# Closer steps for the second query group's norm, and an edge on the first head's key splits

## The chip, the cores and the metric

The kernel runs on one core of one Trainium2 chip. The metric is the device time of one execution in microseconds (us), and the comparison is with the same kernel before the change. The engines go by the profile's names: PE (TensorE, matmuls and transposes), PEld (its weight loads), DVE (VectorE), ACT (ScalarE), POOL (GpSimd) and SP (the queue that issues most transfers).

## What is computed

One layer of a hybrid encoder over 512 tokens and 16 meta tokens, width 2048, in float32. A projection of the normalised input feeds two mixers of eight heads each. Mixer B is differential attention with a distance penalty. Mixer A is grouped-query attention whose queries and keys are normalised per head and then turned by a rotary table. Cut to what matters here:

```python
hn = rmsnorm(h, pre_norm_g)
qa, ka, va, ga, qb, kb, vb, gb = split(hn @ w_in)
# mixer A: 8 query heads, 2 key heads
q = axial_rope(rmsnorm(heads_first(qa), q_norm_g), ang_row, ang_col)
k = axial_rope(rmsnorm(heads_first(ka), k_norm_g), ang_row, ang_col)
ya = softmax(q @ k.T / sqrt(128)) @ v * silu(ga)
yb = diff_attention(qb, kb, vb) * silu(gb)
out = h + rmsnorm(concat(ya, yb) @ w_out, post_norm_g)
```

## The kernel before

Every float32 operand is split into a high part (rounded to the matmul's input type) and a low part (the rest), and a product is three matmuls: high by high, low by high, high by low. `wsplit` (lines 155 to 161) does it for a block of 128x1024 weights: ACT writes `wh` (line 158), DVE writes `wl` (line 159). Blocks are fetched two ahead of the one in use, and each of `st`, `wh` and `wl` has three buffers, so the split of a block waits until PE has done with the block three before it. `hi` (line 322, ACT) and `lo` (line 325, DVE) do the same for activations.

PE's order is written out by the program itself. The dense projections form the main stream (`pd` tiles, and `po` tiles for the output projection). Attention heads are generators that the class `Lanes` (line 44) weaves into it. It keeps a clock that advances by an estimate of each matmul's time; a generator that yields x is taken up again when that clock has moved on by x. So a number after `yield` sets how many matmuls stand between two steps of a head, and through that where everything after it stands. `finish` runs a generator to its end at once, without other matmuls between, if it has not got there by then. On PE and SP the instructions stay in program order; on DVE, ACT and POOL a scheduler orders them, and each engine then takes them strictly one after the other.

Mixer A comes late. `queries_A(g)` (line 663) projects the queries of group g, four heads, into four token tiles `qn` (128 tokens by four heads by 128). For the second group, g = 1, the norm is the generator `later` (line 688): for each tile four squares with a sum on ACT (`jk`, line 596), then `rstd` on POOL (`ssq`, lines 243 and 245), and then for each tile on DVE four gain products (`gains`, line 601) and four operations of the rotation (`rope`, lines 618 to 623). They run while heads 2 and 3 of the first group are at work and while the gates `gA` are projected.

`attention_A(h)` (line 541) for the first head of the second group, h = 4, waits until that generator has ended (line 542). Then PE transposes the four tiles of the head (`tr<-ident,qn`, line 549), ACT and DVE split the result (`qh`, `qlA`), and four times PE computes scores (`sc`, line 566), DVE adds and takes the minimum (line 570), ACT takes the exponential (line 573) and POOL scales (line 575). `p_times_v` (line 414) transposes two blocks of scores (`tr<-ident,p`), splits them (`ph`, `pl`, `pm`) and multiplies with the values (`pv`). The transposes and `pv` share two PSUM banks, `sc` has one buffer. Heads 4 to 7 follow each other; the last is forced to its end at the last block of the first output projection (`dense_out(0)`, line 860), whose operand `oh15`, `ol15` is its result. The gate's SiLU (line 394) and the exponential need different tables on ACT, so each change between them has an ACT_TABLE_LOAD.

`keys_B` (line 327) of the first head of mixer B stands much earlier, behind the projection that opens the main stream (line 785): `halves` scales the keys, `hi` and `lo` split them into `s1` and `s2`.

Of the kernel before, what the change touches and what calls it, by code (L numbers as in the profile page):

```python
# [2 lines left out]

# [1 line left out]

# [5 lines left out]
F32 = mybir.dt.float32  # L11
F32R = mybir.dt.float32r
F16 = mybir.dt.float16
AF = mybir.ActivationFunctionType
ALU = mybir.AluOpType
# [16 lines left out]
LAG = dict(vals=3.5, bank=2.8, bankA=1.5, bankB=2.5, turnA=1.5, turnB=1.5, pvA=2.6, pvB=4.0, scB=3.0,  # L32
           pB=8.0, ss=6.0, qA=2.35, scA=5.4, pA=4.14, rope=10.2, head=3.85, fin=1.35, qn=1.4, norm=4.0)
# [75 lines left out]
def kernel(ctx: ExitStack, tc: tile.TileContext, xT, xn, xm, w_s, w_t, w_q, w_o,  # L109
                             gpre, gq, gk, lams, gsub, gpost, ident_d, cos_d, sin_d, dist_d, out):  # L110
    nc = tc.nc
# [43 lines left out]
    def wsplit(st, c=slice(0, 1024), ws=None):  # L155
        wh, wl = ws or [wp.tile([P, 1024], F32R, name=n, tag=n) for n in ("wh", "wl")]
        with tc.high_priority(rank[0]):
            nc.scalar.activation(wh[:, c], st[:, c], AF.Copy)  # L158
            nc.vector.tensor_tensor(out=wl[:, c], in0=st[:, c], in1=wh[:, c].bitcast(F32),  # L159
                                    op=ALU.subtract)  # L160
        return wh, wl

    rank = [AHEAD]

# [59 lines left out]
    first = [[pd.tile([P, 512], F32, name="pd", tag="pd") for _ in segs] for segs in start]  # L224
    for k0 in range(0, KT, 2):
        xload(k0)
        wh, wl = wload(w_s[k0 // 2], 768, load, 2 if k0 == 0 else 1)
        xload(k0 + 1)
        for k in (k0, k0 + 1):
            for i, (segs, pss) in enumerate(zip(start, first)):  # L230
                c = slice((i + 3 * (k - k0)) * P, (i + 3 * (k - k0) + 1) * P)
# [24 lines left out]
    for t in (TT, 0, 1, 2, 3):  # L256
        rows = P if t < TT else NM
        src = xn[t * P:(t + 1) * P, :] if t < TT else xm
        for j in range(2 if t < 2 else 4):
# [4 lines left out]
            st = ap.tile([P, w], F32, name="xns", tag=tag, bufs=2 if t < 2 else 4)[:rows]  # L264
# [54 lines left out]
    L, U = slice(0, 64), slice(64, 128)  # L319

    def hi(dst, src):
        nc.scalar.activation(dst, src, AF.Copy)  # L322

    def lo(dst, src, h):
        nc.vector.tensor_tensor(out=dst, in0=src, in1=h.bitcast(F32), op=ALU.subtract)  # L325

    def keys_B(pss):
        kf = ap.tile([P, NT], F32, name="kf", tag="tT")
        halves(pss, kf)
        s1 = ap.tile([P, NT], F32R, name="s1", tag="s1")  # L330
        s2 = ap.tile([P, NT], F32R, name="s2", tag="s2")
        hi(s1[L], kf[L])
        hi(s2[U], kf[U])
        lo(s1[U], kf[L], s1[L])
        lo(s2[L], kf[U], s2[U])
        return s1, s2

# [325 lines left out]
    def queries_A(g):  # L663

        pss = [pd.tile([P, 512], F32, name="pd", tag="pd") for _ in range(TT)]
        for k0 in range(0, KT, 2):
            wh, wl = fetch()

            for k, ts in [(k, h) for h in ((0, 1), (2, 3)) for k in (k0, k0 + 1)]:
                c = slice((k - k0) * 512, (k - k0 + 1) * 512)  # L670
                for t in ts:
                    ts_ = slice(NM + t * P, NM + (t + 1) * P)
                    mm(pss[t], xh[k][:, ts_], wh[:, c], start=(k == 0), stop=False)
                    mm(pss[t], xl[k][:, ts_], wh[:, c], start=False, stop=False)
                    mm(pss[t], xh[k][:, ts_], wl[:, c], start=False, stop=(k == KT - 1))
                    lanes.poll()
        res = []
        for t in range(TT):
            tag = "ql" if g == 0 else "fr" if t < 2 else "f"
            qn = ap.tile([P, 4, P], F32, name="qn", tag=tag, bufs=2 if tag == "fr" else 4)  # L680
            nc.scalar.activation(qn.rearrange("p n d -> p (n d)"), pss[t], AF.Copy,
                                 scale=rt[:, t:t + 1])
            res.append(qn)

        def last_of(engine):
            return next(i for i in reversed(nc.cur_bb.bb.instructions) if i.engine == engine)

        def later():

            ss = ap.tile([P, 16], F32, name="ssq", tag="ssq", bufs=1)  # L690
            for t, qn in enumerate(res):
                squares(qn, 4, ss[:, 4 * t:4 * t + 4])
                yield 2.0
            rstd(ss, ss, P)
            yield LAG["norm"]
            for t, qn in enumerate(res):
                with tc.issue_after(last_of(mybir.EngineType.DVE)):
                    gains(qn, 4, gqB, ss[:, 4 * t:4 * t + 4])
                    rope(qn, cosT[:, t:t + 1, :].broadcast_to([P, 4, P]),
                         sinT[:, t:t + 1, :].broadcast_to([P, 4, P]))  # L700
                yield LAG["norm"]

        def turn():
            if g == 1:
                yield from later()
                return
            for t, qn in enumerate(res):
                head_norm(qn, 4, gqB)
                rope(qn, cosT[:, t:t + 1, :].broadcast_to([P, 4, P]),
                     sinT[:, t:t + 1, :].broadcast_to([P, 4, P]))  # L710
                yield LAG["norm"]

        return res, lanes.spawn(turn(), 0.0)
# [69 lines left out]

    sc = psc.tile([P, 2, 512], F32, name="sc", tag="sc")
    pss = dense_T(KEYS, [sc[:, 0, :], sc[:, 1, :]], spread)
    ks = keys_B(first[0])
    qs = queries_B(0, first[1])
    v = values(pss)
    gB = [gate(first[2], "gB0")] + [None] * (NH - 1)
# [6 lines left out]
    for h in range(NH):  # L796
# [4 lines left out]
        if h + 1 < NH:  # L801
            if h:
                weigh()
            pss = dense_T(KEYS)
# [8 lines left out]
    for i in range(2):  # L813
        pss = dense_T(KEYS)
# [337 lines left out]
```

## Time and profile before

| what | value |
|---|---|
| median of 3 runs | 928.04 us (927.98 to 929.32) |
| the profiled execution | 927.7 us |
| its span (first to last instruction) | 925.9 us |
| mean granted clock of PE | 0.998 |
| busy: PE, DVE, ACT, POOL | 98%, 62%, 52%, 12% of the span |

In a row of the timeline the first number is the start in us from the span's start and the second the duration; "x4" means four instructions in one row, and brackets at the end name idle time before the row and what ended it. Matmuls are pipelined, so a matmul's duration is longer than its distance to the next one; distances between starts tell what PE's stream costs. In a row of windows the columns are: stretch, its length, busy time and number of instructions of PE, PEld, DVE, ACT and POOL, granted clock, share of the DMA engines, GB/s. In a row that groups a line's instructions the last numbers are busy us, mean ns of one, and idle time before them.

### The profile page before, as it was taken

The page shows a single profiled execution, that of the slowest core. Times are in us where ns is not written, and L with a number is a line of the kernel's source. Part 1 is how long each engine was busy: PE and PEld are TensorE (multiplying, and loading weights), DVE is VectorE, ACT ScalarE, POOL GpSimd, SP SyncE. Part 2 cuts the span into 40 slices and gives each one's busy share as a digit, 9 for nine tenths or more (in the row PEclk, how much of TensorE's full clock was granted, in tenths as well). Part 3 has the DMA queues.
Part 4 walks back from the last instruction along what each step waited for, and adds up shares of the span by engine and source line. Part 5 has one row for each costly group of instructions (what it writes and reads, how often), then busy time and mean ns, then how long its engine had stood idle before and what let it go on. Part 6 is the DMA issues. An engine that isn't in the chain of part 4 may idle for free.

```text
span 925.9 us, 14235 instructions
## 1 busy us (share of the span) xinstructions
PE 911.5 (98%) x5498; PEld 808.3 (87%) x5498; DVE 577.0 (62%) x1029; ACT 484.8 (52%) x847; POOL 114.1 (12%) x158
## 2 busy tenths in 40 slices
PE   9999999999999999999999999999999999899995
PEld 8999898998989899898999888888888888788884
DVE  6676675847567575765756247444755664564797
ACT  6464564638455474644655254437536753524652
POOL 0101010110101110010110020113101120300110
PEclk9999999999999999999999999999999999999999
DMA  9844534644536364232223223222222352676974
GB/s 340 286 137 140 148 113 113 156 130 142 143 108 178 93 169 137 69 104 69 91 64 98 91 91 91 69 80 80 73 88 68 121 157 80 230 218 185 298 305 182
DMA packets 43893, 128.11 MB, mean 138 GB/s; under 512 B 5105, under 2 KB 9073, under 8 KB 43569
## 3 DMA queue, kind: packets, MB, share of 16 engines
q1 hardware_dynamic: 40416, 115.66, 37.3%
q0 software_dynamic: 3264, 11.54, 6.6%
q8 instruction: 43, 0.70, 0.3%
q14 instruction: 26, 0.20, 0.1%
q10 hardware_dynamic: 144, 0.01, 0.0%
HBM read 118.80 MB, written 25.17 MB: 155 GB/s over the span
## 4 chain that ended last, share of the span: by engine, by line
PE 95%; DVE 3%; issue 0%; ACT 0%; POOL 0%; DVEq 0%
PE pd L63 61%; PE po L63 17%; PE sc L63 7%; PE pv L63 5%; PE tr L66 5%; DVE y L1041 1%; DVE wl L159 1%; PE hot L63 0%; PE ss L63 0%; DVE y L1053 0%; DVE y L1047 0%; DVE pl L325 0%; DVE l L325 0%; POOL p L490 0%; ACT ph L322 0%
## 5 line engine op out<-in xcount | busy, mean ns | idle before, releaser
L63 PE MATMUL pd<-xh,wh 128*128 128x264 f32 (+1 forms) x992 | 331.8, 335 | 0.0
L63 PE MATMUL pd<-xh,wl 128*128 128x264 f32 (+1 forms) x992 | 323.1, 326 | 1.2 <-DVE wl L159 1.2
L63 PE MATMUL pd<-xl,wh 128*128 128x264 f32 (+1 forms) x992 | 323.1, 326 | 0.0
L158 ACT ACTIVATE wh<-st 128x1024 fp32r<-128x1024 f32 (+2 forms) x147 | 152.9, 1040 | 207.2 <-issue 91.8
L159 DVE TENSOR_TENSOR wl<-st,wh 128x1024 fp32r<-128x1024 f32 (+2 forms) x147 | 176.5, 1202 | 115.0 <-ACT wh L158 114.2
L63 PEld LDWEIGHTS pd<-xh,wl 128*128 128x128 f32 x992 | 186.6, 188 | 17.5 <-DVE wl L159 1.6
L63 PEld LDWEIGHTS pd<-xh,wh 128*128 128x128 f32 x992 | 187.1, 189 | 11.8 <-ACT wh L158 0.2
L63 PEld LDWEIGHTS pd<-xl,wh 128*128 128x128 f32 x992 | 187.3, 189 | 10.7
L63 PE MATMUL po<-wh,oh 128*128 128x512 f32 x176 | 69.5, 398 | 1.2 <-ACT oh L322 1.2
L485 ACT ACTIVATE p<-p,mx 128x528 f32<-128x528 f32 x64 | 46.9, 734 | 43.7 <-DVE mx L477 43.4
L63 PE MATMUL po<-wh,ol 128*128 128x512 f32 x176 | 68.3, 391 | 0.2 <-DVE ol L325 0.2
L63 PE MATMUL po<-wl,oh 128*128 128x512 f32 x176 | 68.3, 391 | 0.0
L322 ACT ACTIVATE ph<-tr 128x512 fp32r<-128x512 f32 x64 | 37.8, 592 | 43.1 <-PE tr L66 42.7
L325 DVE TENSOR_TENSOR pl<-tr,ph 128x512 fp32r<-128x512 f32 x64 | 43.4, 687 | 18.7 <-ACT ph L322 18.3
L477 DVE CUSTOM_DVE_ANT_0 p<-sc,dist 128x528 f32<-128x528 f32 x64 | 44.9, 701 | 11.7 <-PE sc L63 11.3
L63 PE MATMUL pd<-wh,xh 128*128 128x512 f32 x128 | 51.6, 403 | 0.0
L66 PE MATMUL tr<-ident,p 128*128 128x128 f32 (+1 forms) x320 | 50.5, 272 | 0.3 <-DVE pl L325 0.3
L63 PE MATMUL pd<-wl,xh 128*128 128x512 f32 x128 | 50.1, 391 | 0.0
L63 PE MATMUL pd<-wh,xl 128*128 128x512 f32 x128 | 50.0, 391 | 0.0
L66 PEld LDWEIGHTS tr<-ident,p 128*128 128x128 f32 (+1 forms) x320 | 37.2, 131 | 10.9 <-DVE pl L325 0.6
L490 POOL TENSOR_SCALAR p<-p,sm 128x528 f32<-128x528 f32 x32 | 23.0, 718 | 170.8 <-DVE sm L487 157.6
L575 POOL TENSOR_SCALAR p<-p,smA 128x528 f32<-128x528 f32 x32 | 25.3, 791 | 141.6 <-DVE smA L574 101.8
(208 smaller groups left out, 1472.2 us busy)
## 6 DMA issues: line engine op xcount, KB each, us to landing
st<-in_w_t_dram SPq DMA_DIRECT2D x82, 512.0 KB, 4.0
st<-in_w_o_dram SPq DMA_DIRECT2D x24, 512.0 KB, 3.7
ws<-in_w_o_dram POOLq DMA_DIRECT2D x16, 512.0 KB, 5.7
st<-in_w_q_dram SPq DMA_DIRECT2D x16, 512.0 KB, 3.6
st<-ws SPq DMA_DIRECT2D x16, 512.0 KB, 4.2
xs<-in_xT_dram SPq DMA_DIRECT2D x16, 264.0 KB, 5.4
ws<-in_w_o_dram SPq DMA_DIRECT2D x8, 512.0 KB, 5.1
ws<-ws SPq DMA_DIRECT2D x8, 512.0 KB, 5.0
```

The source lines that it names most:

```text
L63: self._add(self.nc.tensor.matmul(out, lhsT, rhs, start=start, stop=stop), us)
L66: self._add(self.nc.tensor.transpose(out, in_, ident), 0.109)
L158: nc.scalar.activation(wh[:, c], st[:, c], AF.Copy)
L159: nc.vector.tensor_tensor(out=wl[:, c], in0=st[:, c], in1=wh[:, c].bitcast(F32), op=ALU.subtract)
L322: nc.scalar.activation(dst, src, AF.Copy)
L325: nc.vector.tensor_tensor(out=dst, in0=src, in1=h.bitcast(F32), op=ALU.subtract)
L477: nc.vector.tensor_tensor_reduce(out=two(p), in0=sc[:, :, :HALF], in1=two(dist[:, w0:w0 + NT]), scale=-0.125 / slope(h), scalar=3.0e38, op ...
L485: nc.scalar.activation(p2[m], p2[m], AF.Exp, scale=-1.0, bias=mx[:, m:m + 1], accum_out=sm[:, m:m + 1])
L490: nc.gpsimd.tensor_scalar(out=p2[0], in0=p2[0], scalar1=sm[:, 0:1], scalar2=1.0, op0=ALU.mult, op1=ALU.mult)
L575: nc.gpsimd.tensor_scalar(out=p, in0=p, scalar1=sm, scalar2=1.0, op0=ALU.mult, op1=ALU.mult)
L1041: order(nc.vector.scalar_tensor_tensor(out=v, in0=v, scalar=ry[t], in1=xres[t, g], op0=ALU.mult, op1=ALU.add))
```

## The change

Two edits. In `later`, the yields of the second group's norm go from 2.0 to 0.8 us behind each tile's squares and from 4.0 (`LAG["norm"]`) to 3.0 behind `rstd` and behind each tile's gains and rotation: 4 x 1.2 + 1 + 4 x 1 = 9.8 us of the lane clock less until head 4 may begin. In `keys_B`, the first head's first `hi` and first `lo` get a scheduling edge each: ACT's `hi(s1)` is issued behind the ACT half, and DVE's `lo(s1)` behind the DVE half, of the split that stands third from the end of the list `splits` when `keys_B` is called. An edge orders instructions of one engine and adds no semaphore.

```diff
     def wsplit(st, c=slice(0, 1024), ws=None):
         with tc.high_priority(rank[0]):
-            nc.scalar.activation(wh[:, c], st[:, c], AF.Copy)
-            nc.vector.tensor_tensor(out=wl[:, c], in0=st[:, c], in1=wh[:, c].bitcast(F32),
-                                    op=ALU.subtract)
+            splits.append((nc.scalar.activation(wh[:, c], st[:, c], AF.Copy),
+                           nc.vector.tensor_tensor(out=wl[:, c], in0=st[:, c],
+                                                   in1=wh[:, c].bitcast(F32), op=ALU.subtract)))
...
-    def keys_B(pss):
+    def keys_B(pss, after=lambda e: nullcontext()):
...
-        hi(s1[L], kf[L])
+        with after(0):
+            hi(s1[L], kf[L])
         hi(s2[U], kf[U])
-        lo(s1[U], kf[L], s1[L])
+        with after(1):
+            lo(s1[U], kf[L], s1[L])
...
             for t, qn in enumerate(res):
                 squares(qn, 4, ss[:, 4 * t:4 * t + 4])
-                yield 2.0
+                yield 0.8
             rstd(ss, ss, P)
-            yield LAG["norm"]
+            yield 3.0
             for t, qn in enumerate(res):
                 with tc.issue_after(last_of(mybir.EngineType.DVE)):
                     gains(qn, 4, gqB, ss[:, 4 * t:4 * t + 4])
                     rope(...)
-                yield LAG["norm"]
+                yield 3.0
...
-    ks = keys_B(first[0])
+    ks = keys_B(first[0], lambda e: tc.issue_after(splits[-3][e].ins))
```

In the changed kernel the lines from `wsplit` on stand two to five lines lower. The order of the instructions on each engine is the same in both kernels up to the second group's norm, the first head's splits included. Those stand on ACT as follows (`s1`, `s2` the keys, `q1`, `q2` the queries, `wh_583` and `wh_637` the next weights; the split third from the end of the list is `wh_467`):

```order
L158 ACTIVATE wh_467<-st_465 128x1024
...
L324 ACTIVATE s1_698<-kf_695 64x528
L310 ACTIVATE lsm_555<-lsm_555 128x2
L324 ACTIVATE s2_699<-kf_695 64x528
L324 ACTIVATE q1_706<-qf_704 64x512
L158 ACTIVATE wh_583<-st_581 128x1024
L324 ACTIVATE q2_707<-qf_704 64x512
L158 ACTIVATE wh_637<-st_635 128x1024
```

So the edge asks for an order that was there already. The first place that moves is on PE at head 4's queries (`qn`). Before, PE goes from the last small transposes of a pair of head 3's scores (`tr_6993`) to 30 dense matmuls, a product with the values and two groups of four transposes of the next scores, and only then to the queries:

```order
L66 MATMUL tr_6993<-ident_531,p_6754 32x128
L63 MATMUL pd_6944<-xh5_116,wh_6782 128x512
...
L63 MATMUL pd_6944<-xl14_141,wh_6860 128x512
L63 MATMUL pd_6944<-xh14_125,wl_6861 128x512
L66 MATMUL tr_7078<-ident_531,qn_6599 128x128
L66 MATMUL tr_7078<-ident_531,qn_6601 128x128
L66 MATMUL tr_7078<-ident_531,qn_6603 128x128
L66 MATMUL tr_7078<-ident_531,qn_6605 128x128
```

Now the same small transposes (here `tr_7002`) are followed by three dense matmuls and then by the queries:

```order
L66 MATMUL tr_7002<-ident_531,p_6762 32x128
L63 MATMUL pd_6953<-xh5_116,wh_6784 128x512
L63 MATMUL pd_6953<-xl5_132,wh_6784 128x512
L63 MATMUL pd_6953<-xh5_116,wl_6785 128x512
L66 MATMUL tr_7013<-ident_531,qn_6599 128x128
L66 MATMUL tr_7013<-ident_531,qn_6601 128x128
L66 MATMUL tr_7013<-ident_531,qn_6603 128x128
L66 MATMUL tr_7013<-ident_531,qn_6605 128x128
```

The queries' transposes have moved forward past a whole product with the values, two groups of transposes and the dense matmuls between them. The end of the norm on DVE, which they read, stands before the change so (`t_7031` is the rotation's work tile of the fourth token tile, `pl` and `pm` belong to head 3's scores):

```order
L601 SCALAR_TENSOR_TENSOR qn<-qn,ssq,gqB 128x128 x3
L580 TENSOR_TENSOR gA_6941<-pv,gA_6941 128x256
L618 TENSOR_TENSOR t_7031<-qn,sinT 128x8x32
L620 TENSOR_TENSOR t_7031<-qn,sinT 128x8x32
L622 TENSOR_TENSOR qn<-qn,cosT 128x512
L325 TENSOR_TENSOR pl<-tr,ph 128x512
L623 TENSOR_TENSOR qn<-qn,t_7031 128x512
```

and after it so:

```order
L327 TENSOR_TENSOR pl<-tr,ph 128x512
L605 SCALAR_TENSOR_TENSOR qn<-qn,ssq,gqB 128x128 x4
L159 TENSOR_TENSOR wl<-st,wh 128x1024
L622 TENSOR_TENSOR t_6981<-qn,sinT 128x8x32
L624 TENSOR_TENSOR t_6981<-qn,sinT 128x8x32
L327 TENSOR_TENSOR pl<-tr,ph 128x512
L626 TENSOR_TENSOR qn<-qn,cosT 128x512
L327 TENSOR_TENSOR pm<-tr,pm 32x256
L627 TENSOR_TENSOR qn<-qn,t_6981 128x512
L327 TENSOR_TENSOR qlA<-tr,qh 128x512
```

The first tile's gains and rotation have moved up, in front of the two `pl` and the weights' split of their neighbourhood; the last tile's still end the norm. The third place is ACT from head 6's queries (`qh`) to the first operands of the output projection (`oh`). Before:

```order
L573 ACTIVATE p,smA<-p,mxA 128x528
L322 ACTIVATE qh<-tr 128x512
L322 ACTIVATE pm<-tr 32x256
L322 ACTIVATE oh_7553<-os 128x512
L322 ACTIVATE oh_7554<-os 128x512
L394 ACT_TABLE_LOAD
L394 ACTIVATE gA_7546<-gA_7546 128x512
L573 ACT_TABLE_LOAD
```

Now head 6's `qh`, and some rows later the first operands:

```order
L158 ACTIVATE wh<-st 128x1024
L398 ACT_TABLE_LOAD
L398 ACTIVATE gA_7427<-gA_7427 128x512
L577 ACT_TABLE_LOAD
L577 ACTIVATE p,smA<-p,mxA 128x528
L324 ACTIVATE qh<-tr 128x512
...
L324 ACTIVATE oh_7594<-os 128x512
L577 ACTIVATE p,smA<-p,mxA 128x528
L398 ACT_TABLE_LOAD
L398 ACTIVATE gA_7587<-gA_7587 128x512
L324 ACTIVATE oh_7595<-os 128x512
```

Head 6's `qh` now stands behind a weights' split, a gate's SiLU, both table loads and an exponential, and the second operand of the output projection stands behind an exponential, a table load and the last gate's SiLU.

More of the change, by code (lines that the diff above doesn't have):

```diff
@@ L1 @@
 import math
-from contextlib import ExitStack
+from contextlib import ExitStack, nullcontext
 import numpy as np
@@ L157, in wsplit @@
         with tc.high_priority(rank[0]):
-            nc.scalar.activation(wh[:, c], st[:, c], AF.Copy)
-            nc.vector.tensor_tensor(out=wl[:, c], in0=st[:, c], in1=wh[:, c].bitcast(F32),
-                                    op=ALU.subtract)
+            splits.append((nc.scalar.activation(wh[:, c], st[:, c], AF.Copy),
+                           nc.vector.tensor_tensor(out=wl[:, c], in0=st[:, c],
+                                                   in1=wh[:, c].bitcast(F32), op=ALU.subtract)))
         return wh, wl
+    splits = []
     rank = [AHEAD]
```

## Prediction

> **What bounds the kernel now.** I read the page first, then who waits for whom on PE, then windows and the timeline around the second group's norm.
>
> ```profile
> span 925.9 us, 14235 instructions
> PE 911.5 (98%) x5498; PEld 808.3 (87%) x5498; DVE 577.0 (62%) x1029; ACT 484.8 (52%) x847; POOL 114.1 (12%) x158
> ```
>
> PE is busy 98% of the span, so its stream sets the time, and an order that changes no matmul can win only waits or add some. The waits of PE, longest first:
>
> ```profile
> PE pd L63 <- DVE wl L159: 1.2, 1, 1.2
> ...
> PE po L63 <- ACT oh L322: 1.2, 1, 1.2
> PE pv L63 <- DVE pl L325: 0.7, 1, 0.7
> PE tr L66 <- DVE pl L325: 0.3, 1, 0.3
> ```
>
> Little is there to be won: one wait near the first head, and 2.2 us in three waits at the forced end of the last head. What an order can lose is seen in the stretch of the norm:
>
> ```profile
> 657.50:678.60 21.10, 21.10 (x119) 17.86 (x118) 20.65 (x47) 7.94 (x13) 2.06 (x3) 1.00 0.27 89
> ```
>
> Here DVE is busy 20.65 of 21.1 us. For 21 us there is a second engine at its limit, and what PE reads from it has no margin.
>
> **Part 1, the edge on the key splits: nothing.** ACT's rows at the first head:
>
> ```profile
> 35.42 1.06 ACT L158 ACTIVATE wh<-st 128x1024 fp32r<-128x1024 f32 x1 [1.49 <-PE pd L63]
> 49.02 0.64 ACT L322 ACTIVATE s<-kf 64x528 fp32r<-64x528 f32 x1 [6.95 <-DVE kf L316]
> 50.99 1.04 ACT L158 ACTIVATE wh<-st 128x1024 fp32r<-128x1024 f32 x1
> ```
>
> Two blocks are fetched ahead, so the last two entries of the list are the blocks split from 50.99 on, and the third from the end is the one at 35.42: that is 13.6 us before `s1` starts. The edge orders what is ordered already, on DVE too, and the built order shows no row moved there. The wait of 1.2 us for `wl` stays. Had the edge named the next block, it could have won at most these 1.2 us.
>
> **Part 2, the norm: the wait at head 4.** The yields take 9.8 us off the clock that lets head 4 in. ACT's squares stay in their places, PE's reading moves forward, and the question is whether DVE's four tiles come forward as far. PE first:
>
> ```profile
> 668.85 0.38 PE L66 MATMUL tr<-ident,p 128*32 128x128 f32 x2
> 668.98 0.48 PE L63 MATMUL pd<-xh,wh 128*128 128x512 f32 x1
> ...
> 677.25 0.60 PE L66 MATMUL tr<-ident,p 128*128 128x128 f32 x4
> 677.61 0.48 PE L63 MATMUL pd<-xh,wh 128*128 128x512 f32 x1
> ...
> 678.39 0.67 PE L66 MATMUL tr<-ident,qn 128*128 128x128 f32 x4
> ```
>
> Three dense matmuls behind transposes take 678.39 - 677.61 = 0.78 us, four transposes 677.61 - 677.25 = 0.36. Up to 668.98 PE's order is unchanged; then the queries stand behind three dense matmuls, at 669.76 in place of 678.39, and the fourth transpose, which reads the fourth tile, at 670.0.
>
> DVE next, where the norm begins, and the stretch before the change from a weights' split to the last addition of the fourth tile:
>
> ```profile
> 653.12 0.42 DVE L580 TENSOR_TENSOR gA<-pv,gA 128x256 f32<-128x256 f32 x1 [0.17 <-PE pv L63]
> 657.58 1.23 DVE L159 TENSOR_TENSOR wl<-st,wh 128x1024 fp32r<-128x1024 f32 x1 [0.25 <-ACT wh L158]
> 677.99 0.68 DVE L623 TENSOR_TENSOR qn<-qn,t 128x512 f32<-128x512 f32 x1
> ```
>
> That is 678.67 - 657.58 = 21.1 us, some 0.3 of it idle. It holds all 16 gains and 16 steps of the rotation, and its end only just meets PE's transposes at 678.39 (they last 0.67, others 0.60). In the changed order the norm begins behind the multiplication at 653.12, so at 653.5, and up to the last addition DVE has the same list but for one `wl` and one `gA` product fewer, one `pl` and one reciprocal more:
>
> ```profile
> L159 DVE TENSOR_TENSOR wl<-st,wh 128x1024 fp32r<-128x1024 f32 x3 | 3.7, 1223 | 0.4 <-ACT wh L158 0.4
> L325 DVE TENSOR_TENSOR pl<-tr,ph 128x512 fp32r<-128x512 f32 x4 | 2.7, 685 | 0.0
> L580 DVE TENSOR_TENSOR gA<-pv,gA 128x256 f32<-128x256 f32 x2 | 0.8, 421 | 0.0
> L574 DVE RECIPROCAL smA<-smA 128x1 f32<-128x1 f32 x1 | 0.2, 156 | 0.0
> ```
>
> 20.8 - 1.22 - 0.42 + 0.69 + 0.16 = 20.0 us, so the fourth tile is done at 673.5. DVE comes forward by 5.2 us, PE by 8.6: **PE waits 3.4 us**, and nothing stands behind these transposes that it could do first. If the list packs better by a gap or two it is 2.6, if DVE is held up by its inputs on the way 4.2.
>
> **The wait at head 6.** In the new order PE reaches head 6's scores as it reached head 5's before (last scores of the old head, three dense matmuls, queries, six value products between two threes of dense ones, scores):
>
> ```profile
> 700.49 0.28 PE L63 MATMUL sc<-kh,qh 128*128 128x264 f32 x1
> ...
> 704.42 0.28 PE L63 MATMUL sc<-kh,qh 128*128 128x264 f32 x1
> 704.54 0.28 PE L63 MATMUL sc<-kl,qh 128*128 128x264 f32 x1
> 704.96 0.39 PE L63 MATMUL sc<-kh,qlA 128*128 128x264 f32 x1
> ```
>
> That takes 704.42 - 700.49 = 3.93 us. Before, ACT had a split and an exponential in that time; `qlA` was 0.3 late (0.42 us between starts where 0.12 is usual). Now the gate's SiLU and two table loads stand in front of `qh`. The chain runs from a weights' split, which waits for PE's last matmul ahead of those scores, and the trace has it once, off PE's path:
>
> ```profile
> 694.33 1.05 ACT L158 ACTIVATE wh<-st 128x1024 fp32r<-128x1024 f32 x1
> 695.40 1.28 ACT L394 ACT_TABLE_LOAD   x1
> 696.69 0.63 ACT L394 ACTIVATE gA<-gA 128x512 f32<-128x512 f32 x1
> 697.34 1.28 ACT L573 ACT_TABLE_LOAD   x1
> 698.64 0.74 ACT L573 ACTIVATE p<-p,mxA 128x528 f32<-128x528 f32 x1
> ...
> 699.37 0.57 ACT L322 ACTIVATE ph<-tr 128x512 fp32r<-128x512 f32 x1
> ...
> 704.23 0.68 DVE L325 TENSOR_TENSOR qlA<-tr,qh 128x512 fp32r<-128x512 f32 x1
> ```
>
> From the split to the next free moment 699.37 - 694.33 = 5.04 us, then `qh` at 0.57 (like the `ph` here): 5.6 against 3.93, so the first score waits 1.7. `qlA` takes 0.68 more, where PE has 0.24 us of work: 0.4 more. **Together 2.1 us**; 1.4 if ACT starts its split a little earlier, 2.8 if DVE has its own split in hand when `qlA` falls due.
>
> The rows show the load alone: SiLU starts 1.29 us behind the load's start. The Trainium skill ("ScalarE: Activation LUTs", What ACT_TABLE_LOAD costs) gives about 1283 ns and adds a drain of about 1380 ns for each switch; by that estimate this wait would be 2.8 us longer and the time 935.0. The trace agrees with the load and shows no drain, so the sum goes by the rows.
>
> **The output projection's second operand.** ACT's rows there before:
>
> ```profile
> 727.09 1.14 ACT L322 ACTIVATE oh<-os 128x512 fp32r<-128x512 f32 x2
> 728.25 1.28 ACT L394 ACT_TABLE_LOAD   x1
> ```
>
> Now a table load and a SiLU (1.94 by the chain above) and an exponential stand between the two `oh`, and PE has 12 matmuls on the first. I estimate 0 to 1.0 us, and take 0.5.
>
> **What is won.** At the end of the last head PE's forced transposes now have dense matmuls between them:
>
> ```profile
> 788.18 0.60 PE L66 MATMUL tr<-ident,p 128*128 128x128 f32 x4
> ...
> 790.20 0.39 PE L63 MATMUL pv<-ph,vh 128*128 128x256 f32 x1 [0.68 <-DVE pl L325]
> ```
>
> Six transposes there took 2.02 us, where 0.36 + 0.13 would do (668.98 - 668.85 is the pair): 1.5 won. The wait for `oh15` behind the last product (1.2) stays, since that product is still forced. With head 5's 0.3 the gain is 1.8.
>
> **What moves along at no cost.** With the heads come POOL's scalings and `pm` copies, on an engine busy 12% of the span, and on SP the spills of the finished heads: head 5's now stands two weight loads earlier, head 6's one, head 7's where it was.
>
> ```profile
> st<-in_w_o_dram SPq DMA_DIRECT2D x24, 512.0 KB, 3.7
> ```
>
> A spill that waits for its head holds up the loads behind it. They land in 3.7 us and are issued about two blocks ahead, and a block lasts PE 24 matmuls, over 5 us; the heads end earlier along with their spills, so I count nothing. Were that cover gone, one late load would cost PE up to those 3.7 us.
>
> **The sum.** 3.4 + 2.1 + 0.5 - 1.8 = +4.2 us. On the profiled execution's 927.7 that is 931.9; the median, 928.04, lies 0.3 above it, so I say **932.2**. With all three waits at their low ends 930.2, at their high ends 934.3. About 0.2% (1.9 us) is what a measurement of this kernel can tell from no change.
>
> **The rivals.**
>
> Only the DVE wait (chance 0.09). If DVE's 3.4 us hold but the ACT chains hide, because the scores of head 6 come later than I count, the sum is 3.4 - 1.8 = +1.6: 929.6. Against it stands that PE's wait at head 4 moves ACT's inputs by as much as PE.
>
> DVE keeps pace (0.09), the other side. Its place is the fourth transpose at 670.0; it decides if the fourth tile is done by then, 3.5 us sooner than my list says, and no wait follows. Then the gain of 1.8 is left: 926.2. For it speaks that PE's stream was free of waits through this stretch before; against it the 20.65 busy of 21.1.
>
> The clock falls (0.08). PE stands still for 3.4 us, and in the end rows of the trace its clock goes when it has nothing to do:
>
> ```profile
> 916.00:918.00 2.00, 0.60 (x3) 0.18 (x1) 2.00 (x4) 0.23 (x1) 0.00 (x0) 1.00 0.61 238
> 920.00:922.00 2.00, 0.00 (x0) 0.00 (x0) 2.00 (x4) 0.00 (x0) 0.00 (x0) 0.88 0.65 249
> ```
>
> PE ended at 916.6, the granted clock fell below 1 only after 920, so 3.4 us should pass; if it does not, and half the clock holds for as long again, 1.7 us are added: 933.9. The Trainium skill ("TensorE: Matmul & The Clock Gate", Why this matters for your kernels) warns of gaps of over about 3 us, after which the clock halves; by that rule the drop comes, by the row it does not.
>
> That the change does not do what it says is no rival for its second half but the forecast: that half moves nothing.
>
> **How the numbers follow.** The forecast has 0.74. The range of 929.4 to 934.4 takes in the sum's low and high ends, the first rival and the clock's, and leaves out the case in which DVE keeps pace. Slower by over 0.2% (above 929.9) is the forecast and the clock: 0.82. Within 0.2% are the first rival and half of the second: 0.13. Faster is the rest, 0.05.
>
> **What would show it.** In the changed profile the row of `tr<-ident,qn` at 670 should have some 3.4 us of idle time on PE put down to DVE `qn`, the scores near 720 to 725 about 2 us put down to ACT `qh`; the waits of `pv` and `tr` for `pl` at the end should be gone, that of `pd` for `wl` at 53 still there. I am wrong if PE's waits for `qn` sum to under 2 us, or if PE's stream between 670 and 790 is as free of waits as before.

## The result and the profile after

| what | before | after |
|---|---|---|
| median of 6 runs each, us | 927.98 (927.36 to 929.32) | 933.60 (932.02 to 934.49) |
| ratio, 95% interval | | 1.0056 (1.0043 to 1.0069) |
| the profiled execution, us | 927.7 | 933.88 |
| its span, us | 925.9 | 932.1 |
| mean granted clock | 0.998 | 0.996 |

The change makes the kernel 0.56% slower, 5.6 us by the medians. The forecast was 932.2 with a range of 929.4 to 934.4. In the profiled executions the span is 6.2 us longer. PE is busy for 2.0 us more than the 911.5 before, and the other 4.2 us are idle time of PE:

```profile
span 932.1 us, 14240 instructions
...
PE 913.5 (98%) x5498; PEld 808.8 (87%) x5498; DVE 576.9 (62%) x1029; ACT 486.9 (52%) x849; POOL 115.3 (12%) x158
```

Who waits for whom on PE, in the changed kernel (its `hi` is L324 and its `lo` L327; the lines of the norm and the heads stand four further down):

```profile
PE tr L66 <- DVE pl L327: 1.6, 1, 1.6
PE sc L63 <- ACT qh L324: 1.6, 1, 1.6
PE pd L63 <- DVE wl L159: 1.2, 1, 1.2
PE tr L66 <- DVE qn L627: 1.2, 1, 1.2
```

Three waits of over 1 us are new, two at head 4 and one at head 6 (smaller ones, for `qlA` and `ol`, come below). The old one for `wl` is unchanged, and those of `pv` and `tr` for `pl` at the last head's end are gone. The first one looks as if it had to do with the transposes' bank. PE's rows at head 4:

```profile
669.59 0.40 PE L63 MATMUL pd<-xh,wl 128*128 128x512 f32 x1
671.62 0.55 PE L66 MATMUL tr<-ident,qn 128*128 128x128 f32 x3 [1.64 <-DVE pl L327]
673.39 0.33 PE L66 MATMUL tr<-ident,qn 128*128 128x128 f32 x1 [1.22 <-DVE qn L627]
673.48 0.48 PE L63 MATMUL pd<-xh,wh 128*128 128x512 f32 x1
```

From the last dense matmul to the next one pass 3.89 us, where one dense step (0.23) and four transposes (0.36) need 0.6, so 3.3 us are lost. DVE's rows (the first gain of the norm, a split of head 3's and the norm's last addition) show why there are two pieces and which one sets the end:

```profile
653.52 1.13 DVE L605 SCALAR_TENSOR_TENSOR qn<-qn,ssq,gqB 128x128 f32<-128x128 f32 x4
...
670.88 0.69 DVE L327 TENSOR_TENSOR pl<-tr,ph 128x512 fp32r<-128x512 f32 x1
...
672.65 0.69 DVE L627 TENSOR_TENSOR qn<-qn,t 128x512 f32<-128x512 f32 x1
```

The `pl` at 670.88 reads a bank of transposes that the new transposes need, and it stands in DVE's list in the middle of the fourth tile's rotation, between its products with the sine and that with the cosine. The fourth tile is done at 673.34, and only then can the fourth transpose run. Had the bank been free, three transposes would have been earlier and the end the same; two experiments below show it so.

ACT and PE at head 6:

```profile
716.71 1.06 ACT L158 ACTIVATE wh<-st 128x1024 fp32r<-128x1024 f32 x1 [2.87 <-issue]
717.78 1.28 ACT L398 ACT_TABLE_LOAD   x1
719.08 0.63 ACT L398 ACTIVATE gA<-gA 128x512 f32<-128x512 f32 x1
719.73 1.28 ACT L577 ACT_TABLE_LOAD   x1
...
721.76 0.57 ACT L324 ACTIVATE qh<-tr 128x512 fp32r<-128x512 f32 x1
```

```profile
720.38 0.39 PE L63 MATMUL pd<-xh,wl 128*128 128x512 f32 x1
722.39 0.39 PE L63 MATMUL sc<-kh,qh 128*128 128x264 f32 x1 [1.62 <-ACT qh L324]
722.62 0.28 PE L63 MATMUL sc<-kl,qh 128*128 128x264 f32 x1
723.11 0.59 PE L63 MATMUL sc<-kh,qlA 128*128 128x264 f32 x1 [0.21 <-DVE qlA L327]
...
724.16 0.63 PE L63 MATMUL pd<-xh,wh 128*128 128x512 f32 x1
724.58 0.63 PE L63 MATMUL pd<-xl,wh 128*128 128x512 f32 x1
```

The chain from split to `qh` takes 721.76 - 716.71 = 5.05 us, and PE loses 2.01 - 0.23 = 1.78 for `qh` and 0.49 - 0.12 = 0.37 for `qlA`. Then something appears that no row of before had between 6.7 and 921.5: dense matmuls stand 0.42 us apart where 0.23 is usual. The windows, cut at the moments at which the granted clock changed and at steps of 3.41 us ahead of them, show the clock in the third column from the right (the first number behind the stretch is its length, the second PE's busy time):

```profile
668.33:671.74 3.41, 1.77 (x10) 1.06 (x9) 3.41 (x9) 0.95 (x3) 1.31 (x1) 1.00 0.08 25
671.74:675.16 3.42, 2.20 (x11) 1.69 (x12) 2.23 (x4) 0.80 (x2) 0.00 (x0) 1.00 0.33 128
719.53:722.94 3.41, 1.75 (x10) 1.07 (x9) 0.74 (x2) 2.77 (x5) 0.70 (x1) 1.00 0.49 154
722.94:726.36 3.42, 3.25 (x10) 2.86 (x11) 1.30 (x5) 0.83 (x2) 0.01 (x1) 0.50 0.02 5
```

For one stretch of 3.41 us the clock is at half, behind a stretch in which PE was busy 1.75 us. At head 4, where PE lost more, it did not fall. In this execution that costs about 1.3 us (worked out below).

At the output projection the second operand is late, as it was foreseen, and by more than the 0.5 us of the estimate:

```profile
740.06 1.07 PE L63 MATMUL po<-wh,ol 128*128 128x512 f32 x4
741.20 0.49 PE L63 MATMUL po<-wh,oh 128*128 128x512 f32 x1
741.92 0.50 PE L63 MATMUL po<-wh,ol 128*128 128x512 f32 x1 [0.23 <-DVE ol L327]
742.26 0.39 PE L63 MATMUL po<-wl,oh 128*128 128x512 f32 x1
```

The four take 0.91 at the usual 0.23 and took 1.14; the next two steps took 0.72 and 0.34: 0.23 + 0.49 + 0.11 = 0.8 us lost.

### The profile page after: what moved, and what is told of

It reads as the page before. It is cut to its first block, busy times and chain, and to the rows that moved or that the text cites. A ratio compares the mean times of both kernels' runs of the same rounds, so it can differ in the third digit from the quotient of the medians.

```text
span 932.1 us, 14240 instructions
## 1 busy us (share of the span) xinstructions
PE 913.5 (98%) x5498; PEld 808.8 (87%) x5498; DVE 576.9 (62%) x1029; ACT 486.9 (52%) x849; POOL 115.3 (12%) x158
## 4 chain that ended last, share of the span: by engine, by line
PE 92%; DVE 5%; issue 1%; ACT 1%; DMA 0%; POOL 0%; DVEq 0%; ACTq 0%
PE pd L63 59%; PE po L63 16%; PE sc L63 7%; PE pv L63 5%; PE tr L66 5%; DVE y L1046 1%; DVE wl L159 1%; DVE qn L605 0%; PE ss L63 0%; DMA gcol<-in_gpre_dram 0%; DVE pl L327 0%; DVE y L1058 0%; DVE qn L626 0%; DVE qn L627 0%; ACT L398 0%
## 5 line engine op out<-in xcount | busy, mean ns | idle before, releaser
L324 ACT ACTIVATE ph<-tr 128x512 fp32r<-128x512 f32 x64 | 37.7, 591 | 37.7 <-PE tr L66 37.5
L327 DVE TENSOR_TENSOR pl<-tr,ph 128x512 fp32r<-128x512 f32 x64 | 43.4, 687 | 15.6 <-ACT ph L324 15.1
L66 PEld LDWEIGHTS tr<-ident,p 128*128 128x128 f32 (+1 forms) x320 | 37.3, 131 | 10.6
```

The lines of the kernel that those rows point to most:

```text
L66: self._add(self.nc.tensor.transpose(out, in_, ident), 0.109)
```

## The experiments

Times of one kernel differ from execution to execution by up to 3 us, and much of that comes from the start, which no edit touches: PE's `tr<-dg,ones_r` starts anywhere from 46.1 to 48.2 us in the 13 traces here. The three latest (47.84, 48.05 and 48.15) are the three in which the granted clock was first full at 9.5 to 10.6 us; in the others it was at 4.3 to 6.7. So two traces are compared from PE's first `tr<-ident,qn` of the last head of the first group on (636.33 before) to the last matmul (916.21): 279.88 us before, 285.71 after. In what follows "the stretch" is this one.

The theory: PE's order moves forward by more than DVE's list for the norm can, and ACT's chain at head 6 is longer than PE's work there; on top of both comes the clock. The rivals: the wait at head 4 goes with PE's shift or with the bank; head 6's queries are late for another reason; the edge has a part in it; the clock is a matter of that one execution.

**The yields without the edge.**

```diff
-    ks = keys_B(first[0], lambda e: tc.issue_after(splits[-3][e].ins))
+    ks = keys_B(first[0])
```

> The change without the edge in keys_B. Theory: the edge orders what is ordered already, so this is the whole change again: PE waits 3.3 us for the second group's queries at head 4, 2.1 us for qh and qlA at head 6, some 0.8 us for oh and ol, and gains 1.8 us at the end of the last head; 932.3 us, and 1.7 us more in an execution in which PE's clock falls for 3.41 us behind one of these waits. On the clock: the records of the changed kernel fit a clock that is judged in fixed stretches of 3.413 us whose phase differs from one execution to the next, so times should lie in groups near 932 and 934. Rival on the edge: it has a part in the time, and without it the time is below 931. Rival on the clock: the fall belongs to the wait at head 6 and comes in every execution; then all times lie near 934.

Measured: 935.28 us (932.43 to 935.70, 5 runs) beside 927.72, ratio 1.0073 (1.0060 to 1.0086). The edge has no part in the loss: without it every engine has the same instructions in the same order, and the time is no shorter. The trace, of the fastest execution, has the same waits and no fall of the clock:

```profile
670.94:674.35 3.41, 1.72 (x9) 1.32 (x10) 2.30 (x5) 0.60 (x1) 0.07 (x1) 1.00 0.42 154
...
718.73:722.14 3.41, 1.84 (x12) 1.28 (x10) 0.69 (x2) 3.37 (x6) 0.10 (x1) 1.00 0.44 150
```

The steps of 3.41 us fall elsewhere here (they are counted back from the clock's fall at the end, 923.52): one of them ends at 722.14, just before the wait for `qh` does (722.19), and has PE busy for 1.84 us, not 1.75. The stretch takes 284.45 us, 4.57 more than before and 1.26 less than in the profile after: the waits alone cost 4.6 us, and the fall of the clock 1.3.

The times were not in the two groups, near 932 and 934, that were expected: three of the five are at 935.3 to 935.7. Their granted clocks are 0.992 and 0.993, where the other two (932.43 and 934.08) have 0.996 and the 55 executions of the kernel before beside these experiments 0.996 to 0.998. One step at half the clock takes 0.0018 off such a mean (1.7 of 933 us), so two falls in each of the three would fit; no trace of them was kept.

**Only the squares' yields, and only the gaps'.** The first edit below is the one, the second, behind `rstd` and behind each tile, the other. Both give PE the same order, matmul for matmul: counted from the stretch's first transpose (637.21 and 638.23), PE stands at head 4's queries 36.90 us later in both. But DVE's first gain starts 17.1 us later in the one (654.34) and 23.6 in the other (661.81).

```diff
-                yield 2.0
+                yield 0.8
```

```diff
-            yield LAG["norm"]
+            yield 3.0
```

> The kernel before with the yields behind the squares at 0.8 and LAG norm (4.0) kept. PE's order brings the queries of head 4 at 673.3 in its own stream, 5.1 us earlier than before. Theory of DVE's list: the norm begins at 653.5 as in the changed kernel and its list, summed by the durations of the trace, takes 21.0 us, so it ends at 674.5 and PE waits about 1.0 us; head 6 comes late enough for its gate; the gain of 1.8 us at the end stays: 927.2 us (926.6 to 928.0). Rival, the wait goes with PE's shift (about half of the change's 9.8 us, so half of 3.3 us): 1.6 us and 927.8. Rival, the SiLU still stands before head 6's queries: 2.1 us more, 929.3.

> The kernel before with the yields behind rstd and behind the tiles at 3.0 and 2.0 kept behind the squares. PE's order is the same, matmul for matmul, as with the squares' yields alone, but DVE begins the norm about 6.5 us later, near 660, with a list of 17.3 us. Theory of DVE's list: it ends near 677.5, PE stands at head 4's queries at 673.3, so PE waits about 4 us: 930.3 us (929.5 to 931.5), and 1.7 us more where the clock falls. Rival, the wait goes with PE's shift: the same time as with the squares' yields alone, 927.8.

Measured: 930.26 us (929.47 to 931.65, 9 runs), ratio 1.0025 (1.0015 to 1.0035), with the squares' yields, and 935.51 us (934.31 to 936.38, 4 runs), ratio 1.0082 (1.0068 to 1.0096), with the gaps'. The wait is as DVE's list has it. First the squares', then the gaps':

```profile
674.11 0.49 PE L66 MATMUL tr<-ident,qn 128*128 128x128 f32 x3
675.75 0.33 PE L66 MATMUL tr<-ident,qn 128*128 128x128 f32 x1 [1.15 <-DVE qn L623]
```

```profile
675.13 0.49 PE L66 MATMUL tr<-ident,qn 128*128 128x128 f32 x3
679.42 0.33 PE L66 MATMUL tr<-ident,qn 128*128 128x128 f32 x1 [3.80 <-DVE qn L623]
```

Here the three first transposes run at once and the fourth waits, 1.3 and 4.0 us (1.0 and "about 4" were expected): where PE's order is the same, what decides is when DVE begins. That the wait goes with PE's shift, or with the bank, is refuted: PE's place is the same in both, and no transpose waits for `pl` here. The times missed their expectations all the same. With the squares' yields the stretch takes 281.70 us, 1.8 more than before where 0.8 less was expected: the queries' low parts and the output projection have new waits that were not counted: 0.8 us for `qlA` (0.50 and 0.56 between starts where 0.12 is usual) and 1.2 for `oh` and `ol`. With the gaps' yields the clock fell behind the wait, as the second row shows, and the stretch takes 286.36:

```profile
676.23:679.64 3.41, 0.21 (x2) 0.22 (x3) 3.07 (x5) 0.00 (x0) 0.00 (x0) 1.00 0.36 112
679.64:683.05 3.41, 3.41 (x13) 2.93 (x13) 0.69 (x1) 1.88 (x2) 0.00 (x0) 0.50 0.14 47
```

**Head 4 held back.**

```diff
                          sinT[:, t:t + 1, :].broadcast_to([P, 4, P]))
                 yield 3.0
+            yield 3.4
```

> The whole change with one more yield of 3.4 us behind the last tile's rotation, so that head 4 starts that much later in PE's order (674.7 in place of 669.8) while the norm itself begins and ends as in the changed kernel (673.3). Theory of DVE's list: PE's wait at head 4 goes to 0, no clock falls, head 6's queries come behind its gate's SiLU with time to spare, oh1 is reached in time, and the gain of 1.8 us at the end of the last head stays: 926.2 us (925.8 to 927.2), faster than before. Rival, DVE's list moves back along with head 4 or other waits take the place: 928 to 930. Rival, the end of the last head needs the whole 9.8 us: 928.0.

Measured: 929.20 us (928.28 to 931.52, 11 runs), ratio 1.0015 (1.0006 to 1.0024): 4 to 6 us better than the change, and still slower than before. The mechanism is as stated: the four transposes stand in one row without a wait.

```profile
675.59 0.60 PE L66 MATMUL tr<-ident,qn 128*128 128x128 f32 x4
```

The time missed its expectation (926.2), and the rival of other waits came true: the gain is eaten by small waits that the new places make. PE loses 0.4 us for `qh` and 0.4 for `qlA` at head 5, 0.2 and 0.4 at head 7, 1.4 in all. The stretch takes 280.10 us, 0.2 more than before. The medians differ by 1.5 us; in the trace, which is of the median execution, 0.95 of it lies ahead of `tr<-dg,ones_r` (47.17, where 46.22 was before) and 0.3 behind the last matmul. Whether the change has a part in that is open.

**The head 6 chain without its SiLU.** The gate of head 6 is copied, so that its SiLU is left out.

```diff
-        nc.scalar.activation(g, g, AF.Silu)
+        nc.scalar.activation(g, g, AF.Copy if name == "gA6" else AF.Silu)
```

> The whole change, with the gate of head 6 copied and its SiLU left out, so that ACT has two table loads fewer (2 x 1.28 us) in front of head 6's qh; the order of all engines is else the same. Theory of ACT's chain: split, copy, exponential and qh take 1.05 + 0.6 + 0.74 + 0.57 = 3.0 us where PE has 3.9 us of work, so the wait for qh (1.8 us) goes and that for qlA stays under 0.4; from the last head of the first group to the last product of head 7 some 157.8 us in place of 159.9, and 2 us off the time: 930 to 932. Rival, qh is late because its transposes or DVE are: the wait stays and the time with it.

Measured: 932.09 us (931.90 to 933.35, 4 runs) beside 928.02. The wait is gone, for `qlA` too, and ACT goes from the split's start to `qh` in 2.44 us where it took 5.05:

```profile
722.30 0.39 PE L63 MATMUL pd<-xh,wl 128*128 128x512 f32 x1
722.53 0.28 PE L63 MATMUL sc<-kh,qh 128*128 128x264 f32 x1
...
722.77 0.28 PE L63 MATMUL sc<-kh,qlA 128*128 128x264 f32 x1
```

The two table loads ahead of `qh` are the wait at head 6. In this execution the clock fell behind head 4 instead, which is why the time is just above the expected upper end (the stretch takes 283.50 us: 284.45, less the 2.15 of this wait, and 1.3 for the fall, make 283.6):

```profile
670.63:674.04 3.41, 0.93 (x5) 0.67 (x6) 2.91 (x6) 0.01 (x1) 0.87 (x1) 1.00 0.45 154
674.04:677.46 3.42, 3.42 (x9) 2.63 (x8) 1.01 (x2) 1.98 (x3) 0.00 (x0) 0.50 0.03 7
```

**PE kept busy in its waits.** Matmuls whose result is overwritten fill the idle time, first in the change, then in the kernel with the gaps' yields alone (22 ahead of head 4).

```diff
+        def fill(n):
+            sc = psc.tile([P, 2, 512], F32, name="sc", tag="sc")
+            for _ in range(n):
+                tc.keep_in_program_order(nc.tensor.matmul(
+                    sc[:, 0, :HALF], k[0][:, :P], k[0][:, :HALF], start=True, stop=True))
+            return [sc]
+        sc0 = fill(11) if h == 4 else []
...
+        if h == 6:
+            sc0 = fill(10)
...
```

> The whole change, and PE gets 11 extra score-sized matmuls ahead of head 4's transposes and 10 ahead of head 6's scores, into a score bank that the next real scores overwrite; at 0.115 us each they take 1.3 and 1.2 us of idle time that PE has there anyway (3.2 and 1.8 us), so the waits end when they ended. Theory of the clock (a stretch of 3.41 us with more than about half of it idle is followed by one at half the clock, and its phase differs from execution to execution): the idle time left in any one stretch is at most some 1.9 us, no fall comes at 670 or 720 in any execution, and the times lie as far above those of the kernel before as the waits make them, 4.5 us: lowest near 932, median 932.4 (931.8 to 933.2), 1 to 2 us under the median of the change without filling (933.6 and 935.3 in two sets of runs). Rival, the falls cost nothing and the scatter is of the start alone: the median is that of the change, 933.6 to 935.3. Rival, the added matmuls come in the way: over 935.

> The gaps' yields alone (3.0 behind rstd and the tiles, 2.0 behind the squares), and PE gets 22 extra score-sized matmuls (22 x 0.115 = 2.5 us) ahead of head 4's transposes, in the 4.0 us that it stands still there; the fourth tile still ends the wait. Theory of the clock: a wait of 4.0 us leaves at least one stretch of 3.41 us more than half idle whatever its phase, so without the filling the clock falls there in every execution (8 matmuls, each 0.2 us longer, 1.6 us); with it 1.5 us are idle, no fall: 933.9 (933.2 to 934.7) where the gaps' yields alone took 935.5. Rival, the fall in that profile was of that execution alone: the median stays at 935.5. Rival, the filling comes in the way of something: over 936.

Measured: the filled change 932.47 us (932.30 to 932.89, 5 runs), ratio 1.0045 (1.0031 to 1.0058); the filled gaps 933.74 (933.11 to 933.86, 4 runs), ratio 1.0059 (1.0044 to 1.0074). More work on PE makes both kernels faster. The filled change is 1.1 us below the change by the medians, which alone would not be clear (the intervals of the two ratios overlap), and 2.8 below the yields alone, which have the change's order; the filled gaps are 1.8 us below the gaps', and no run of the one reaches one of the other. In the traces the stretch is 1.5 us shorter (284.20) and 1.2 us (285.16). The waits end where they ended (in the change the fourth transpose 37.0 us and head 6's first score 86.0 us behind the stretch's start, filled or not), but PE's busy time in the steps is up, and the clock stays. First two rows of the filled change, then the emptiest step of the filled gaps' wait:

```profile
668.36:671.78 3.42, 3.42 (x22) 2.79 (x20) 3.42 (x9) 1.42 (x3) 1.32 (x1) 1.00 0.01 2
...
719.56:722.97 3.41, 3.00 (x22) 2.62 (x20) 0.66 (x3) 3.23 (x5) 0.24 (x1) 1.00 0.43 151
```

```profile
674.95:678.36 3.41, 2.25 (x19) 1.98 (x18) 2.84 (x5) 0.08 (x1) 0.00 (x0) 1.00 0.44 129
```

So it is not one execution's matter: the granted clock is 0.994 or 0.995 in all four executions with the gaps' yields and 0.996 to 0.998 in all four of the filled ones. Of the six of the change, the three slowest are the one whose trace shows the fall (933.88) and two at 0.995 (934.21 and 934.49). The runs of the filled kernels also lie closer together, but five and four are too few to show that.

**The rotation's sine products on POOL.** `rope` takes an engine for its products with the sine, and the norm of the second group gives it POOL.

```diff
-        nc.vector.tensor_tensor(out=t2[:, :, :, 0:32], in0=xv[:, :, :, 32:64],
+        eng.tensor_tensor(out=t2[:, :, :, 0:32], in0=xv[:, :, :, 32:64],
...
```

> The whole change, with the eight products with the sine (t, lines 622 and 624 of the changed kernel, 0.34 us from start to start on DVE) given to POOL; PE's and ACT's orders stay. Theory of DVE's list: its list from the first gain to the last addition falls by 2.7 us to 17.1, it ends at 670.6 where PE needs the fourth tile at 670.0, and the wait at head 4 goes from 3.2 us to about 0.7 (0.5 to 2.0, since POOL's products may be slower than DVE's, 0.76 us for its 128x528 scaling, and each tile then waits for them): 2.5 us less than the change, 930.0 without a fall of the clock, 929 to 931.5. Rival, the bank of the transposes that the profile names (1.6 us put down to pl): that part stays and only 1.2 us go, 931.5. Rival, POOL is so slow that the wait stays or grows: 933 or more.

Measured: 938.84 us (937.11 to 940.27, 4 runs), ratio 1.0115 (1.0101 to 1.0129). The expectation failed and the last rival holds. POOL takes longer for a product than DVE, and DVE, which takes its list in order, stands waiting for it. A row of POOL's and one of DVE's:

```profile
656.52 0.75 POOL L623 TENSOR_TENSOR t<-qn,sinT 128x256 f32<-128x256 f32 x1 [5.95 <-DVE qn L605]
```

```profile
657.99 0.69 DVE L627 TENSOR_TENSOR qn<-qn,cosT 128x512 f32<-128x512 f32 x1 [1.55 <-POOL t L625]
```

DVE was relieved of 8 x 0.34 = 2.7 us and waited for POOL four times (1.55, 1.33, 0.63 and 0.99 by the brackets, 4.5 in all). Beside that, operations of the two engines that ran at once were slower: DVE's cosine product at 666.96 took 1.22 us where 0.69 is usual, POOL's product at 667.59 took 1.18 where 0.73 is. As the list's end decides, PE's wait grew, to 2.1 us for `gA` at head 3's transposes and 2.0 for `qn` at head 4, and the clock fell three times. It says nothing against DVE's list as the cause: the list got longer, and PE's wait with it.

**The edge at the place that its words name, and the tail alone.** The first kernel is that of before with edges on all `hi` and `lo` of the first head, to the split second from the end. The third changes only the lag ahead of the value products; the second is both.

```diff
...
+    qs = queries_B(0, first[1], lambda e: tc.issue_after(splits[-2][e].ins))
...
-        yield LAG["pv" + ab]
+        yield LAG["pv" + ab] - (0.6 if gate_of in (5, 6, 7) else 0.0)
```

> The kernel before with the edge that the change's second half names, placed as its words have it: all of the first head's hi stand behind ACT's half of the split second from the end of the list (the block that PE takes up at 52.7), all of its lo behind DVE's half. Theory: the change's own edge had no effect because it named the block before; with this one wl stands ahead of DVE's four lo and PE's wait of 1.2 us for it is gone or under 0.3: 1.0 us off the time, 926.9 where the kernel before has 927.9. Rival, the block's transfer lands too late: the wait turns into one for wh and the time stays. Rival, the first head comes late and PE waits for its scores instead: 928 to 930.

> The edges of the run before, the yields of the norm as before the change, and the yield ahead of the value products 0.6 us shorter for heads 5 to 7 (2.0 in place of 2.6), which brings head 7's end far enough forward that its last transposes are no longer forced. Theory: the change's gain at the end (1.3 us in the traces) does not need an earlier norm; with it and the edges the time is 2.2 us below the kernel before: 925.7 (925.2 to 926.9). Rival, the shorter lag makes PE wait for pl in each product: 927 to 929.

> The kernel before, with the yield ahead of the value products 0.6 us shorter for heads 5 to 7 and nothing else: no edges, the norm's yields as before. Theory: head 7's end is free of forced transposes, 1.2 us less (1.3 won, 0.1 to 0.3 for other waits), with head 1's wait for wl of 1.2 us still there: 926.8 (926.3 to 927.5), and the edges' part of the run with both (926.5) was near nothing since the waits for vf and the scores took the place of that for wl. Rival, the edges carried it: 928.0 here.

Measured: the edges 928.22 us (927.02 to 929.64, 11 runs), ratio 1.0001 (0.9992 to 1.0010); edges and tail 926.52 (925.97 to 927.69, 11 runs), ratio 0.9983 (0.9974 to 0.9992); the tail alone 927.12 (926.29 to 929.47, 11 runs), ratio 0.9991 (0.9982 to 1.0000). With the edges the wait for `wl` is gone, and one for `vf` takes most of its place:

```profile
PE tr L66 <- DVE vf L318: 0.7, 1, 0.7
```

`vf` stands behind the low parts in DVE's list, and these came later (the last one ends at 57.17, where it ended at 56.83). In its trace PE is 0.3 us ahead by the last head of the first group, and loses 0.8 at head 7's scores, where it waits for `mxA`. The gain of the edges alone was not found in the time. With the shorter lag the end of the last head is as in the change, with dense matmuls behind the last transposes and no wait there but that for the last `oh`, without an earlier norm:

```profile
788.12 0.38 PE L66 MATMUL tr<-ident,p 128*32 128x128 f32 x2
...
789.73 0.28 PE L63 MATMUL pv<-ph,vh 128*128 128x256 f32 x1
```

Edges and tail together are the one version that is clearly faster than before, by 0.17%; the stretch takes 278.70 us there, 1.2 less. Of the tail alone the interval reaches 1, and its trace, of its slowest execution, shows no gain in the stretch (280.09): PE has a new wait of 1.6 us ahead of 753.9, put down to `gA`. By ACT's and DVE's rows it goes back to a late transfer, for which ACT waits 3.05 us here and 1.1 with edges and tail:

```profile
745.80 1.16 ACT L322 ACTIVATE oh<-os 128x512 fp32r<-128x512 f32 x2 [3.05 <-DMA os<-oscr]
```

Whether the edges keep that transfer in time or this execution was unlucky is open, and so is how much of the gain is the tail's alone.

## Why the prediction was right, and where it was not

The time lies in the range, on the forecast's side. Point by point:

- **The edge moves nothing: right.** The wait for `wl` is 1.2 us as before, and the yields alone lose as much as the whole change.
- **Head 4, 3.4 us: right, 3.3 measured.** By the letter of the sign that was named (waits for `qn` of under 2 us) it would have failed, since the profile puts only 1.2 down to `qn` and 1.6 to `pl`, whose place in the fourth tile's list was not in the prediction; the sign was badly chosen, as the lost time between the dense matmuls is what counts. DVE begins at 653.5 and ends at 673.3, where 653.5 and 673.5 were worked out. The two kernels with one PE order and two starts of the norm show that it is DVE's list.
- **Head 6, 2.1 us: right, 2.15 measured**, with a chain of 5.05 us where 5.04 was read from a place off PE's path. Copying the gate takes the wait away. The changes of table cost no more than the loads here: SiLU starts 1.30 us behind the first load's start (717.78 and 719.08), and the second load 0.02 us behind SiLU's end.
- **The output projection, 0.5 us: 0.8 measured**, inside its bounds.
- **The gain, 1.8 us: right.** The waits above come to 3.3 + 2.15 + 0.8 = 6.25 us; the stretch without a fall of the clock is 4.57 longer, so 1.7 were won. That is a difference of sums; no row shows it as such.
- **The sum, +4.2 us: 4.6 measured** in the execution in which the clock did not fall. (The three high ends add up to 934.2, not 934.3.)
- **The clock: wrong.** The step that failed is the rival's weight of 0.08, with the sentence that 3.4 us should pass, since at the end of the trace of before PE ended at 916.6 and the clock fell only after 920. That delay is no property of the gap. Steps of 3.413 us run through the whole execution: in the profile after, the clock is full for 716.80 us, half for 3.413 and full for 201.39, which are 210, 1 and 59 steps, and in that of before it is full for 914.77 us, 268 steps. The clock of one step goes with PE's busy time in the step ahead (the last section has the figures). The end rows of before say the same when they are cut at these steps:

```profile
914.68:918.10 3.42, 1.92 (x9) 1.26 (x7) 3.38 (x7) 0.42 (x2) 0.00 (x0) 1.00 0.61 237
918.10:921.51 3.41, 0.00 (x0) 0.00 (x0) 3.38 (x7) 0.68 (x3) 0.00 (x0) 1.00 0.62 239
921.51:924.93 3.42, 0.00 (x0) 0.00 (x0) 1.00 (x2) 0.00 (x0) 0.00 (x0) 0.50 0.76 294
```

The step in which PE ended still counted as busy, so that the fall came a step later. The rival's price (1.7 us) was nearly right, at 1.3 us; its place was not, since in the profile after the clock fell behind the shorter wait, at head 6. The falls would account for most of the 1.4 us by which the median, 933.6, stands above the forecast: with the waits filled the change takes 932.47.

The Trainium skill ("TensorE: Matmul & The Clock Gate", What's actually happening) gives a window of 3413 ns that runs freely, which agrees with the steps measured here; its rule that the clock falls after an idle window does not: 1.75 us busy of 3.41 were too few.

## What to carry to other kernels

When a step is moved ahead on one engine, compare how far the engine that feeds it can follow: the wait is the difference of the two shifts, and where an engine is at 98% of a stretch (20.65 of 21.1 us) its list can be added up from rows (here to 0.2 us). Ask of each place that is passed on the way which engine changes its table there. A stall of about 2 us or more on PE is not always paid only once: it can halve the clock of the next 3.4 us, in some executions and not in others, and here 10 to 22 useless matmuls in a wait were cheaper than the falls.

## What the hardware showed that was not expected

The clock changes in steps of 3.413 us that do not start with the kernel: it was first full anywhere from 4.3 to 10.6 us, and from there on each trace keeps to its own steps. Of the steps at the full clock in the 13 traces, those with PE busy for at most 1.45 us were followed by one at half the clock (0.21, 0.93, 1.35 and 1.45 us within the kernels, 0 to 1.22 at their ends), those with 1.76 us or more by none. Between them it went either way: behind 1.58 and 1.75 it fell, behind 1.72, and behind 1.56 at the ends of two traces, it did not. Busy times are partly modelled, and the exact border is open. A wait of 2 us is therefore sometimes free of a second price and sometimes not, by where a step ends. The kernel with POOL's products shows it three times in one execution; this is the last of them, at head 6:

```profile
726.75:730.16 3.41, 1.58 (x9) 1.13 (x9) 0.94 (x3) 1.75 (x4) 0.70 (x1) 1.00 0.46 150
730.16:733.57 3.41, 3.41 (x12) 2.82 (x11) 1.19 (x4) 0.85 (x3) 0.70 (x1) 0.50 0.23 82
```

And a product of 128x256 elements whose rows are read in pieces of 32 takes 0.72 to 0.78 us on POOL, when it runs undisturbed, where DVE takes 0.42.
